# U's second half with every tile 512 columns wide: 16 narrow matmuls of each pair become 8 wide ones

## The chip, the core and the metric

The kernel runs on one core of one Trainium2 chip. The metric is device microseconds (us) of that core, lower is better. TensorE (PE) multiplies, its weight loads are listed apart as PEld; ScalarE (ACT), VectorE (DVE) and the DMA queue of SyncE (SP) stand beside it. Each engine executes its instructions in the order in which the built program lists them, and waits at an instruction until the semaphores that this instruction names have been raised.

## The reference, cut to what matters

A decoder layer with a mixer, and then a PEER layer over 16384 one-neuron experts, for 256 tokens. Only the last lines matter here:

```python
u = expert_u[eidx]
act = gelu(einsum('td,thkd->thk', xc, u))
out = einsum('thk,thkd->td', g * act, expert_v[eidx])
```

The kernel computes this densely: it multiplies x by every row of U, takes the GELU, multiplies by a gate that is zero for experts that a token has not chosen, and multiplies the result by V.

## The kernel before, in words

U is 16384 x 1024. It is read in 128 tiles of 128 experts by 1024 inputs, 512 KB each. A tile is computed as the sum of three products, because x and U are each split into a rounded high part and a low remainder: U_hi x_hi, U_hi x_lo and U_lo x_hi. The inputs go in eight chunks of 128, so one product is eight matmuls with 256 columns, one column for each token. The array `x2` holds the high and the low part of x side by side, 512 columns for each chunk.

There are two ways to do a tile.

- `dense` does 24 matmuls of 256 columns into one half of a PSUM bank: U_hi with x_hi, U_hi with x_lo, U_lo with x_hi.
- `u_wide` does U_hi with both halves of x at once: seven matmuls of 512 columns, then eight of 256 columns for U_lo with x_hi, then the eighth of 512 columns. The U_hi x_lo part then stands in the second half of the bank. ACT copies it to `ul` in SBUF, and DVE adds it to the first half.

The tiles of the first half (64, experts 0 to 63 of each group) all use `u_wide`. The second half is a loop of 32 pairs, n = 0 to 31. In a pair the even tile (r = 0) goes through `dense` straight into `pt[:, 0]`, and the odd tile (r = 1) through `u_wide` into a bank of its own, from which the add writes `pt[:, 1]`. Then ACT takes the GELU of `pt` in two pieces, and DVE multiplies one of them by the gates that are already in `act[1]`.

`gates(g, n)` makes the gates of eight tokens. DVE makes the one-hot rows `o1`, `eq` and `eq` times the gate weight; ACT makes eight scaled copies (line 1135), one for each token; PE multiplies 16 times (line 1141), two matmuls for each token, of which the second needs that token's scaled copy. DVE then multiplies the gates into `act[0]` and into the finished part of `act[1]` (line 1147), and ACT copies the rest (line 1149). There are 32 such groups. `spread` gives two to pair 0, two to pair 15, none to pairs 30 and 31, and one to each other pair. In the loop they are called in the middle of the even tile, between the U_hi and the U_lo matmuls.

All of this is written as a program without order across engines. A list scheduler of the framework places the instructions of each engine. PSUM has four banks for U tiles (`pbank`), and two for gates (`gbank`). `eq` has one buffer, `o1` and `o2` two, the split tiles `hi` and `lo` three, and `ul` one.

Of the kernel before, what the change touches and what calls it, by code (L numbers as in the profile page):

```python
# [20 lines left out]
T = 256  # L21
# [20 lines left out]
def f32(ap):  # L42
    return ap.bitcast(F32)
# [10 lines left out]
def layer(ctx, tc, I, out, tap=None, upto=None):  # L54
    nc = tc.nc
    V, S, P, PE = nc.vector, nc.scalar, nc.gpsimd, nc.tensor
# [5 lines left out]
    def load(src):  # L62
        raw = stream.tile([128, 1024], F32, tag="raw", bufs=RAWB, name="raw")
        nc.sync.dma_start(raw, src.rearrange("p a b -> p (a b)") if len(src.shape) == 3 else src)
        return raw

    def split(raw, eng=V, hi=None, lo=None):
        if hi is None:
            hi = stream.tile([128, 1024], F32R, tag="hi", bufs=HIB, name="hi")
            lo = stream.tile([128, 1024], F32R, tag="lo", bufs=LOB, name="lo")  # L70
        S.copy(hi, raw)  # L71
        eng.tensor_tensor(lo, raw, f32(hi), op=OP.subtract)  # L72
        return hi, lo

    def split3(raw):
        hi, lo = (stream.tile([128, 1024], F32R, tag=t, bufs=n, name=t)
                  for t, n in (("hi", HIB), ("lo", LOB)))
        S.copy(hi, raw)  # L78
        return hi, lo, V.tensor_tensor(lo, raw, f32(hi), op=OP.subtract)  # L79
# [22 lines left out]
    def pbank(shape):  # L102
        return ps.tile(shape, F32, tag="w", bufs=4, name="pw")
# [4 lines left out]
    def abank(shape):  # L108
        return ps0.tile(shape, F32, tag="a", bufs=2, name="pa")
# [3 lines left out]
    with ExitStack() as px:  # L113
# [6 lines left out]
        with ExitStack() as mx:  # L120
# [16 lines left out]
            pt = pbank([128, 512])  # L137
# [634 lines left out]
            for k in (4, 5, 6, 7):  # L772
                if k == 5:
                    r = sb.tile([128, 2, 1024], F32R, tag="qk", name="W5")
                    W[k] = split(load(I["w_out"][:, k, :]), V, r[:, 0], r[:, 1])
                elif k in LATE:
                    r = W3[:, 2 * (k - 6):2 * (k - 6) + 2]
# [7 lines left out]
            for k in range(2):  # L785
                r = sb.tile([128, 2, 1024], F32R, tag="Kin", name="W1") if k else W3[:, 0:2]
# [13 lines left out]
            xh, xl = x2[:, :, 0], x2[:, :, 1]  # L800
# [42 lines left out]
            for q in range(4):  # L843
# [6 lines left out]
                if q < 2:  # L850
                    r = late.tile([128, 2, 1024], F32R, tag="W4", bufs=2, name="W4")
                    hi, lo = r[:, 0], r[:, 1]
                else:
                    hi, lo = (stream.tile([128, 1024], F32R, tag=t, bufs=n, name=t)
                              for t, n in (("hi", HIB), ("lo", LOB)))
# [47 lines left out]
    HALF = NK // 2  # L903
# [4 lines left out]
    def of_tile(half, i):  # L908
        return act[half][:, i // 2, :, i % 2]

    def u_wide(i, dst, pt, pool, bufs):


        hi, lo, low = split3(load(I["u"][i]))
        for d in range(ND - 1):
            PE.matmul(pt, hi[:, 128 * d:128 * d + 128], x2[:, d], start=d == 0, stop=False)  # L916
        for d in range(ND):
            PE.matmul(pt[:, 0], lo[:, 128 * d:128 * d + 128], xh[:, d], start=False, stop=False)  # L918
        PE.matmul(pt, hi[:, D - 128:], x2[:, ND - 1], start=False, stop=True)  # L919
        ul = pool.tile([128, T], F32, tag="ul", bufs=bufs, name="ul")  # L920
        S.copy(ul, pt[:, 1])  # L921
        V.tensor_tensor(dst, pt[:, 0], ul, op=OP.add)  # L922
        return low


    with ExitStack() as rx:
# [24 lines left out]
        for hc in range(4, 16):  # L951
            raw = load(I["w_q"][hc])
            if hc == 4:
                with tc.issue_after(w4dma.ins):
                    nc.sync.dma_start(keys, I["keys"])
            hi, lo = (stream.tile([128, 1024], F32R, tag=t, bufs=n, name=t)
                      for t, n in (("hi", HIB), ("lo", LOB)))
# [4 lines left out]
            pt = abank([128, 2, T])[:, 0]  # L962
# [14 lines left out]
        def gbank(shape):  # L977
            return ps2.tile(shape, F32, tag="g", bufs=2, name="pg")
# [70 lines left out]
        def weigh():  # L1049

            S.activation(df, df, AF.Exp)
            for _ in range(2):
                yield
            sm = sb.tile([128, 2, 8], F32, name="sm")
            V.tensor_reduce(sm, df, axis=AX.X, op=OP.add)
            V.reciprocal(sm, sm)
            V.tensor_tensor(gn.rearrange("p b (h k) -> p b h k", k=16), df,
                            sm[:, :, :, None].to_broadcast([128, 2, 8, 16]), op=OP.mult)
            yield
            for b in range(2):  # L1060
                pt = gbank([128, 3, 128])
                for i, s in enumerate((i1n, i2n, gn)):
                    PE.transpose(pt[:, i], s[:, b], ident)
                sl = slice(128 * b, 128 * b + 128)
                V.tensor_copy(i1T[:, sl], pt[:, 0])
                V.tensor_copy(i2T[:, sl], pt[:, 1])

                gr = sb.tile([128, 128], F32, tag="gr", bufs=1, name="gr")
                V.tensor_scalar(gr, pt[:, 2], GSC, None, op0=OP.mult)
                V.tensor_copy(gT[:, sl], gr)  # L1070
                V.tensor_sub(gL[:, sl], gr, gT[:, sl])
                if tap:
                    tap(f"i1n{b}", i1n[:, b]); tap(f"gn{b}", gn[:, b])
                yield
# [3 lines left out]
        steps, last = chain(route(0), route(1)), weigh()  # L1078
# [18 lines left out]
    gk = ctx.enter_context(tc.tile_pool(name="gk", bufs=1))  # L1097
# [19 lines left out]
    def gates(g, done):  # L1117
        t0 = GT * g
        t = slice(t0, t0 + GT)

        sh = [128, GT // 2, 128, 2]
        o1 = gk.tile(sh, F16, tag="o1", bufs=2, name="o1")
        eq = gk.tile(sh, F16, tag="eq", bufs=1, name="eq")
        o2 = gk.tile([128, 2] + sh[1:], F16, tag="o2", bufs=2, name="o2")
        io = iotaq[:, None].to_broadcast(sh)

        def over(x):
            return x.rearrange("p (a b) -> p a b", b=2)[:, :, None, :].to_broadcast(sh)

        V.tensor_tensor(o1, io, over(i1T[:, t]), op=OP.is_equal)  # L1130
        V.tensor_tensor(eq, io, over(i2T[:, t]), op=OP.is_equal)  # L1131
        V.tensor_tensor(o2[:, 0], eq, over(gT[:, t]), op=OP.mult)

        for i in range(GT):
            S.activation(o2[:, 1, i // 2, :, i % 2], eq[:, i // 2, :, i % 2], AF.Copy,  # L1135
                         scale=gL[:, t0 + i:t0 + i + 1])

        pt = gbank([128, GT, 128])
        for i in range(GT):
            for k in range(2):  # L1140
                PE.matmul(pt[:, i], o1[:, i // 2, :, i % 2], o2[:, k, i // 2, :, i % 2],  # L1141
                          start=k == 0, stop=k == 1)
        gp = pt.rearrange("p t (i r) -> p t i r", r=2)
        for h, n in ((0, HALF // 2), (1, done)):
            if n:
                a = act[h][:, 0:n, t].rearrange("p i t r -> p t i r")
                V.tensor_tensor(a, gp[:, :, HALF // 2 * h:HALF // 2 * h + n], a, op=OP.mult)  # L1147
        if done < HALF // 2:
            S.copy(act[1][:, done:, t].rearrange("p i t r -> p t i r"), gp[:, :, HALF // 2 + done:])

    def spread(n, total, done):

        return min(total, -(-total * (n + 1) // done))

    made = 0
    for n in range(HALF // 2):

        due = spread(n, T // GT, HALF // 2 - 2)

        pt = pbank([128, 2, T])  # L1160
        hi, lo = split(load(I["u"][HALF + 2 * n]))
        dense(PE, pt[:, 0], hi, lo, xh, xl, beside=lambda: [gates(g, n) for g in range(made, due)])
        made = due
        u_wide(HALF + 2 * n + 1, pt[:, 1], pbank([128, 2, T]), gk, 1)
        a = act[1][:, n].rearrange("p t r -> p r t")
        m1 = GT * made
        if m1 < T:
            S.activation(a[:, :, m1:], pt[:, :, m1:], AF.Gelu_apprx_tanh)
        raw = gk.tile([128, T, 2], F32, tag="ga", bufs=2, name="ga").rearrange("p t r -> p r t")
        S.activation(raw[:, :, :m1], pt[:, :, :m1], AF.Gelu_apprx_tanh)  # L1170
        V.tensor_tensor(*(x[:, :, :m1].rearrange("p r t -> p t r") for x in (a, a, raw)), op=OP.mult)
# [39 lines left out]
    last, st = [], {}  # L1211
# [34 lines left out]
    for n, (c0, c1) in enumerate(PIECES):  # L1246
        p = pbank([128, 256]) if n else acc[1][:, 0]
        for i in range(LAST):
            hi, lo, wh, wl = last[i]
# [4 lines left out]
    ln_apply(1, 256, PIECES)  # L1254


def dense(PE, pt, hi, lo, xh, xl, last=None, beside=None):

    order = [(hi, xh), (hi, xl), (lo, xh)]
    if last is xl:  # L1260
        order = [(hi, xh), (lo, xh), (hi, xl)]
    for n, (w, x) in enumerate(order):
        for d in range(ND):
            PE.matmul(pt, w[:, 128 * d:128 * d + 128], x[:, d], start=n == 0 and d == 0,  # L1264
                      stop=n == 2 and d == ND - 1)
        if beside is not None and n == 1:
            beside()


def stats(nc, pool, st, b, z, n=512):  # L1270
# [90 lines left out]
```

## Time and profile before

| what | us |
|---|---|
| median of three runs | 951.42 (950.58 to 951.55) |
| profiled execution, its own time | 949.16 |
| span of that execution in the trace | 947.4 |
| PE busy, share of the span | 934.4, 99% |
| second half of U, from 375.70 to 589.40 | 213.70 |

The trace begins with the mixer. The first half of U ends at 375.70, the second half at 589.40, and V follows. The rows below are from the chain of waits, from the timeline and from groups of instructions; a number such as 1.61 stands for microseconds, where a row names ns it says so.

### The profile page before, as it was taken

The numbers are of one execution on the slowest core, as the hardware profiler recorded it, in microseconds if no ns is written. First come the engines' busy times: TensorE is split into PE (matmuls) and PEld (weight loads), VectorE is DVE, ScalarE is ACT, GpSimd is POOL, SyncE is SP. The second block draws the span as 40 slices with busy tenths as digits, with TensorE's granted clock in tenths as the row PEclk, the third lists the DMA queues.
The fourth block names the chain that finished last, engine by engine and source line by source line (L and its number), as shares of the span: only waits on it lengthen the run. The fifth ranks groups of instructions, "written<-read, shape, count | busy, mean of one in ns | idle before, by whom it ended". The sixth has DMA issues, their size and how long they took to land.

```text
span 947.4 us, 15305 instructions
## 1 busy us (share of the span) xinstructions
PE 934.4 (99%) x5588; PEld 810.0 (86%) x5588; DVE 721.7 (76%) x1495; ACT 562.8 (59%) x1067; POOL 11.2 (1%) x19
## 2 busy tenths in 40 slices
PE   9999999999999999999999999999999999999996
PEld 4887889998888888999999999888888888888885
DVE  9998687998988967888898996655555555555566
ACT  4526644566575667998888776554455465445550
POOL 3000010000000000000000000000000000000000
PEclk9999999999999999999999999999999999999998
DMA  7331573356555555354444445655555585555551
GB/s 290 111 113 58 173 237 112 135 179 202 195 180 198 182 195 178 134 182 156 156 157 156 157 157 178 198 189 192 198 192 190 196 285 188 193 200 189 191 198 45
DMA packets 50075, 166.18 MB, mean 175 GB/s; under 512 B 5328, under 2 KB 9936, under 8 KB 49872
## 3 DMA queue, kind: packets, MB, share of 16 engines
q1 hardware_dynamic: 50000, 165.20, 51.3%
q8 instruction: 44, 0.72, 0.3%
q14 instruction: 31, 0.25, 0.1%
HBM read 163.09 MB, written 2.10 MB: 174 GB/s over the span
## 4 chain that ended last, share of the span: by engine, by line
PE 91%; DVE 8%; issue 1%; ACT 0%; DVEq 0%; ACTq 0%
PE pg L1180 36%; PE pw L916 16%; PE pw L1264 10%; PE pw L918 10%; PE pg L1141 3%; PE pa L1264 3%; PE pw L919 2%; PE pw L768 2%; PE psb L217 1%; PE pa L871 1%; PE pw L623 1%; PE pw L498 1%; PE psb L552 1%; PE pw L648 1%; PE pw L945 0%
## 5 line engine op out<-in xcount | busy, mean ns | idle before, releaser
L72 DVE TENSOR_TENSOR lo<-raw,hi 128x1024 fp32r<-128x1024 f32 x168 | 205.6, 1224 | 151.8 <-ACT hi L71 151.6
L71 ACT CAST hi<-raw 128x1024 fp32r<-128x1024 f32 x168 | 176.9, 1054 | 171.8 <-PE pg L1180 156.5
L1180 PE MATMUL pg<-hi,wv 128*128 128x512 f32 x988 | 264.5, 389 | 0.0
L1180 PEld LDWEIGHTS pg<-hi,wv 128*128 128x128 f32 x988 | 185.4, 188 | 38.7 <-DVE wv L1111 0.2
L916 PE MATMUL pw<-x,hi 128*128 128x512 f32 x672 | 171.2, 393 | 0.0
L1180 PE MATMUL pg<-lo,wv 128*128 128x512 f32 x494 | 152.3, 389 | 0.0
L916 PEld LDWEIGHTS pw<-x,hi 128*128 128x128 f32 x672 | 124.3, 189 | 23.2
L79 DVE TENSOR_TENSOR lo<-raw,hi 128x1024 fp32r<-128x1024 f32 x96 | 117.1, 1219 | 16.8 <-ACT hi L78 15.8
L918 PEld LDWEIGHTS pw<-x,lo 128*128 128x128 f32 x768 | 104.8, 190 | 7.4
L1180 PEld LDWEIGHTS pg<-lo,wv 128*128 128x128 f32 x494 | 92.7, 188 | 19.2
L918 PE MATMUL pw<-x,lo 128*128 128x256 f32 x768 | 107.3, 282 | 0.0
L78 ACT CAST hi<-raw 128x1024 fp32r<-128x1024 f32 x96 | 101.2, 1054 | 4.2 <-PE pa L1264 2.7
L921 ACT COPY ul<-pw 128x256 f32<-128x256 f32 x96 | 35.6, 371 | 90.1 <-PE pw L919 90.1
L1135 ACT ACTIVATE o<-eq,gL 128x128 f16<-128x128 f16 x256 | 84.3, 439 | 6.0 <-DVE eq L1131 5.4
L1264 PEld LDWEIGHTS pw<-x,hi 128*128 128x128 f32 x512 | 65.9, 189 | 1.3
L1264 PE MATMUL pw<-x,hi 128*128 128x256 f32 x512 | 66.6, 283 | 0.0
L1110 ACT CAST wv<-act 128x256 fp32r<-128x256 f32 x125 | 52.3, 419 | 0.8 <-DVE act L1147 0.8
L1111 DVE TENSOR_TENSOR wv<-act,wv 128x256 fp32r<-128x256 f32 x125 | 52.0, 417 | 0.0
L1264 PE MATMUL pw<-x,lo 128*128 128x256 f32 x256 | 38.8, 292 | 0.0
L919 PE MATMUL pw<-x,hi 128*128 128x512 f32 x96 | 38.0, 396 | 0.0
L1141 PE MATMUL pg<-o,o 128*128 128x128 f16 x512 | 36.5, 219 | 0.0
L922 DVE TENSOR_TENSOR us<-pw,ul 128x256 f32<-128x256 f32 x64 | 26.8, 418 | 11.7 <-ACT ul L921 10.9
(341 smaller groups left out, 1121.0 us busy)
## 6 DMA issues: line engine op xcount, KB each, us to landing
raw<-in_u SPq DMA_DIRECT2D x128, 512.0 KB, 3.5
raw<-in_v SPq DMA_DIRECT2D x128, 512.0 KB, 3.4
raw<-in_w_q SPq DMA_DIRECT2D x12, 512.0 KB, 4.1
raw<-in_w_in SPq DMA_DIRECT2D x8, 512.0 KB, 6.2
raw<-in_w_out SPq DMA_DIRECT2D x8, 512.0 KB, 4.1
w<-in_w_in SPq DMA_DIRECT2D x7, 512.0 KB, 8.5
raw<-in_w_q SPq DMA_DIRECT2D x8, 256.0 KB, 4.9
raw<-in_w_glu SPq DMA_DIRECT2D x2, 512.0 KB, 3.4
```

Of the source, the lines that this page charges most:

```text
L71: S.copy(hi, raw)
L72: eng.tensor_tensor(lo, raw, f32(hi), op=OP.subtract)
L78: S.copy(hi, raw)
L79: return hi, lo, V.tensor_tensor(lo, raw, f32(hi), op=OP.subtract)
L916: PE.matmul(pt, hi[:, 128 * d:128 * d + 128], x2[:, d], start=d == 0, stop=False)
L918: PE.matmul(pt[:, 0], lo[:, 128 * d:128 * d + 128], xh[:, d], start=False, stop=False)
L919: PE.matmul(pt, hi[:, D - 128:], x2[:, ND - 1], start=False, stop=True)
L1110: S.copy(wh, of_tile(half, i))
L1135: S.activation(o2[:, 1, i // 2, :, i % 2], eq[:, i // 2, :, i % 2], AF.Copy, scale=gL[:, t0 + i:t0 + i + 1])
L1141: PE.matmul(pt[:, i], o1[:, i // 2, :, i % 2], o2[:, k, i // 2, :, i % 2], start=k == 0, stop=k == 1)
L1180: PE.matmul(acc[b][:, c], x[:, tk], w[:, 512 * c:512 * c + 512], start=first and j == 0, stop=last and j == 2)
L1264: PE.matmul(pt, w[:, 128 * d:128 * d + 128], x[:, d], start=n == 0 and d == 0, stop=n == 2 and d == ND - 1)
```

## The change

The even tile goes through `u_wide` as well. `u_wide` gets an argument `beside`, which is called behind its seven wide matmuls, and the gates of the pair are made there. Each pair now takes three PSUM banks for tiles (`pt` and one for each tile), where it took two. `dense` loses its argument `beside`.

```diff
-    def u_wide(i, dst, pt, pool, bufs):
+    def u_wide(i, dst, pt, pool, bufs, beside=None):
         hi, lo, low = split3(load(I["u"][i]))
         for d in range(ND - 1):
             PE.matmul(pt, hi[:, 128 * d:128 * d + 128], x2[:, d], start=d == 0, stop=False)
+        if beside:
+            beside()
         for d in range(ND):
             PE.matmul(pt[:, 0], lo[:, 128 * d:128 * d + 128], xh[:, d], start=False, stop=False)
         PE.matmul(pt, hi[:, D - 128:], x2[:, ND - 1], start=False, stop=True)
...
         pt = pbank([128, 2, T])
-        hi, lo = split(load(I["u"][HALF + 2 * n]))
-        dense(PE, pt[:, 0], hi, lo, xh, xl, beside=lambda: [gates(g, n) for g in range(made, due)])
+        for r in range(2):
+            u_wide(HALF + 2 * n + r, pt[:, r], pbank([128, 2, T]), gk, 1,
+                   (lambda: [gates(g, n) for g in range(made, due)]) if r == 0 else None)
         made = due
-        u_wide(HALF + 2 * n + 1, pt[:, 1], pbank([128, 2, T]), gk, 1)
...
-        if beside is not None and n == 1:
-            beside()
```

The lines of the changed kernel stand two further on: 918 becomes 920, 921 becomes 923, 1135 becomes 1137, 1141 becomes 1143, 1149 becomes 1151.

First place: PE at the start of the second half. Line 1264 before, and 916 to 921 after, are tile matmuls; `o_4124` and `o_4157` are the one-hot rows of the first and the second group before, `o_4116` and `o_4149` those after. Rows of the same group that only repeat are left out at "...". Before:

```order
L1264 MATMUL pw<-x_1230,hi 128x256 x16
L1141 MATMUL pg<-o_4126,o_4124 128x128
...
L1264 MATMUL pw<-x_1230,lo 128x256 x4
L1141 MATMUL pg<-o_4159,o_4157 128x128
L1264 MATMUL pw<-x_1230,lo 128x256 x4
L1141 MATMUL pg<-o_4159,o_4157 128x128
...
L916 MATMUL pw<-x_1230,hi 128x512
L1141 MATMUL pg<-o_4159,o_4157 128x128
...
L916 MATMUL pw<-x_1230,hi 128x512 x3
```

After:

```order
L916 MATMUL pw<-x_1230,hi 128x512 x7
L1143 MATMUL pg<-o_4118,o_4116 128x128
...
L920 MATMUL pw<-x_1230,lo 128x256 x7
L1143 MATMUL pg<-o_4151,o_4149 128x128
...
L920 MATMUL pw<-x_1230,lo 128x256
L921 MATMUL pw<-x_1230,hi 128x512
L1143 MATMUL pg<-o_4151,o_4149 128x128
...
L916 MATMUL pw<-x_1230,hi 128x512 x7
```

Before, the second group's matmuls were mixed with those of the odd tile; now nine of them stand in the even tile, and the other seven between the even tile and the odd one, all ahead of the odd tile's first matmul.

Second place: ACT in the same stretch, in the changed kernel, from the GELU of the first half's last pair (line 989) to the third and fourth group (`o2_4241`, `o2_4332`). `ul_4191` and `ul_4282` are the copies of the even tiles of pairs 0 and 1, `ul_4217` that of pair 0's odd tile.

```order
L989 ACTIVATE act0_1460<-us_4029 128x2x256
L1137 ACTIVATE o2_4151<-eq_4150,gL_66 128x128 x6
L1151 COPY act1_4097<-pg_4130 128x8x32x2
L1137 ACTIVATE o2_4151<-eq_4150,gL_66 128x128 x2
L923 COPY ul_4191<-pw_4102 128x256
...
L1137 ACTIVATE o2_4241<-eq_4240,gL_66 128x128 x7
L923 COPY ul_4217<-pw_4194 128x256
L1137 ACTIVATE o2_4241<-eq_4240,gL_66 128x128
L78 CAST hi_4319<-raw_4317 128x1024
L1169 ACTIVATE act1_4097<-pw_4101 128x2x240
L1171 ACTIVATE ga_4221<-pw_4101 128x2x16
L1137 ACTIVATE o2_4332<-eq_4331,gL_66 128x128 x6
L923 COPY ul_4282<-pw_4225 128x256
```

In the kernel before, a cast (`L78 CAST hi_4296`) stood between the GELU and the second group's copies; the copies of the even tiles, `ul_4191` and `ul_4282`, are new, and on PE 15 matmuls of the fourth group have moved ahead of pair 1's odd tile.

Third place: ACT in pair 26, late in the loop, in the changed kernel. `ul_6526` is the copy of the tile before, `ul_6591` the new copy of this pair's even tile, `o2_6641` a group of gates of which PE takes the first ten matmuls between this pair's even and odd tile.

```order
L923 COPY ul_6526<-pw_6503 128x256
L78 CAST hi_6628<-raw_6626 128x1024
L1169 ACTIVATE act1_4097<-pw_6442 128x2x32
L1171 ACTIVATE ga_6530<-pw_6442 128x2x224
L1137 ACTIVATE o2_6641<-eq_6640,gL_66 128x128 x2
L1151 COPY act1_4097<-pg_6562 128x8x6x2
L1137 ACTIVATE o2_6641<-eq_6640,gL_66 128x128 x2
L923 COPY ul_6591<-pw_6534 128x256
L1137 ACTIVATE o2_6641<-eq_6640,gL_66 128x128 x4
```

The fifth scaled copy of the group has moved behind the even tile's copy; before, a group's matmuls stood in the middle of the even tile of its own pair, behind eight finished scaled copies.

## Rows read from the trace of the kernel before

**Rows 1.** The page: span, and busy time of each engine.

```profile
span 947.4 us, 15305 instructions
PE 934.4 (99%) x5588; PEld 810.0 (86%) x5588; DVE 721.7 (76%) x1495; ACT 562.8 (59%) x1067; POOL 11.2 (1%) x19
```

**Rows 2.** The page: the chain that ended last, by engine.

```profile
PE 91%; DVE 8%; issue 1%; ACT 0%; DVEq 0%; ACTq 0%
```

**Rows 3.** Windows of eight pairs: stretch, length, busy of PE, PEld, DVE, ACT, POOL, clock, DMA.

```profile
394.70:447.93 53.23, 53.23 (x450) 50.17 (x449) 47.59 (x77) 48.90 (x124) 0.00 (x0) 1.00 0.50 170
501.07:554.29 53.22, 53.22 (x449) 50.16 (x449) 48.71 (x73) 43.07 (x113) 0.00 (x0) 1.00 0.46 159
```

**Rows 4.** Chain of waits in order of time: start, us, what; one pair, and the end.

```profile
390.85 1.92 PE pw L1264 x16
392.77 0.94 PE pg L1141 x16
393.70 1.00 PE pw L1264 x8
394.70 1.61 PE pw L916 x7
396.32 0.95 PE pw L918 x8
397.27 0.23 PE pw L919
...
578.06 2.88 PE pw L1264 x24
...
589.40 50.79 PE pg L1180 x224
```

**Rows 5.** The same chain, the first two pairs of the second half.

```profile
375.70 1.91 PE pw L1264 x16
...
381.78 0.29 PE pw L916
...
383.98 2.28 PE pw L1264 x19
```

**Rows 6.** Timeline of ACT and DVE at the start: start, us, engine, line.

```profile
377.28 0.68 DVE L1131 TENSOR_TENSOR eq<-iotaq,i2T 128x1024 f16<-128x1024 f16 x1
377.69 0.68 ACT L987 ACTIVATE act<-us 128x512 f32<-128x512 f32 x1
378.26 1.03 ACT L78 CAST hi<-raw 128x1024 fp32r<-128x1024 f32 x1
378.82 0.68 DVE L1147 TENSOR_TENSOR act<-pg,act 128x512 f32<-128x512 f32 x1
385.30 0.60 ACT L1168 ACTIVATE act<-pw 128x480 f32<-128x480 f32 x1
```

**Rows 7.** Timeline of ACT and DVE in later pairs.

```profile
390.94 0.37 ACT L921 COPY ul<-pw 128x256 f32<-128x256 f32 x1 [0.26 <-PE pw L919]
391.35 0.43 DVE L922 TENSOR_TENSOR pw<-pw,ul 128x256 f32<-128x256 f32 x1
416.19 1.91 ACT L1135 ACTIVATE o<-eq,gL 128x128 f16<-128x128 f16 x6
418.20 1.06 ACT L71 CAST hi<-raw 128x1024 fp32r<-128x1024 f32 x1
419.15 0.54 ACT L1168 ACTIVATE act<-pw 128x400 f32<-128x400 f32 x1
```

**Rows 8.** The page: the scaled copies, busy us, mean ns of one, idle before.

```profile
L1135 ACT ACTIVATE o<-eq,gL 128x128 f16<-128x128 f16 x256 | 84.3, 439 | 6.0 <-DVE eq L1131 5.4
```

**Rows 9.** Groups by form on ACT, late pairs: shape, count, busy us, mean ns.

```profile
L1170 ACT ACTIVATE ga<-pw 128x448 f32<-128x448 f32 x1 | 0.6, 589 | 0.0
L1168 ACT ACTIVATE act<-pw 128x80 f32<-128x80 f32 x1 | 0.2, 240 | 0.0
L1149 ACT COPY act<-pg 128x96 f32<-128x96 f32 x1 | 0.2, 245 | 0.0
```

More of the change, by code (lines that the diff above doesn't have):

```diff
@@ L1254, in layer, with dense @@
     ln_apply(1, 256, PIECES)
-def dense(PE, pt, hi, lo, xh, xl, last=None, beside=None):
+def dense(PE, pt, hi, lo, xh, xl, last=None):
     order = [(hi, xh), (hi, xl), (lo, xh)]
```

## The prediction, made before the changed kernel ran

> **What bounds the kernel now.** I read the page first: PE is busy for 934.4 of 947.4 us [rows 1], and the chain that ended last is 91% PE [rows 2]. So PE's time is the kernel's time, and the question is how PE's chain in the second half of U gets shorter or breaks. The chain in order of time shows a pair there as six unbroken pieces [rows 4]: 16 narrow matmuls 1.92, 16 gate matmuls 0.94, eight narrow 1.00, seven wide 1.61, eight narrow 0.95, one wide 0.23, together 6.65. The reader should see that no piece waits. The windows show why this is fragile: in eight pairs (53.23 us) DVE is busy for 47.59 to 48.71 and ACT for 48.90 early and 43.07 late [rows 3], so both stand at 81 to 92%, and both execute in order.
>
> **What the change saves on PE.** A narrow matmul costs 1.92 / 16 = 0.120, a wide one 1.61 / 7 = 0.230 [rows 4]. A wide one does the columns of two narrow ones for 0.01 less. By pair: the odd tile takes 1.61 + 0.95 + 0.23 = 2.79, and an even tile without gates takes 2.88 [rows 4]; both now take 2.79.
> Not all of it stays. Where a wide matmul follows gate matmuls it takes 0.29 in place of 0.23 [rows 5], and the eight narrow ones behind gates take 1.00 in place of 0.95. In the new order a group is often cut into two blocks, one in the even tile and one ahead of the odd one; I count 48 blocks. Sum for the stage without any wait: 64 tiles x 2.79 = 178.6, 32 groups x 0.94 = 30.1, 48 x 0.06 = 2.9, together 211.5. Now it is 589.40 - 375.70 = 213.70 [rows 4, 5]. The saving is **2.2 us**.
> Here the Trainium skill can be weighed. The page "TensorE: Matmul & The Clock Gate", section "Back-to-back issue gap", gives a gap of N / 2.4 + 2.5 ns for a matmul of N columns, 109 ns for 256 and 216 ns for 512. An estimate by that page would be 16 x 109 - 8 x 216 = 16 ns for a pair, 0.5 us in all, in place of 2.2. The rows give 0.120 and 0.230, so the trace stands above both figures, and I keep the rows.
>
> **What it adds beside PE.** Each even tile gets a copy `ul` on ACT (0.37) and an add on DVE (0.43) [rows 7], 32 of each. By engine time there is still room: ACT 48.90 / 8 + 0.37 = 6.48 early, DVE 48.71 / 8 + 0.43 = 6.52 late, against 211.5 / 32 = 6.61 for PE. So on average they stay hidden, with almost nothing to spare. The third PSUM bank costs nothing by itself: the odd tile's bank was last freed by an add of the pair before, the even one's by the GELU of the pair before, which ends some 2 us behind the pair, and PE can take only the older one of these a whole tile later.
>
> **What moves.** The order shows the real cost. Gates of the next pair now stand on PE between the even tile and the odd one. A gate matmul that waits for its scaled copy holds back the whole odd tile, where before the eight scaled copies were finished long ahead. What is late next is ACT's queue: casts, GELUs and the new copy stand ahead of the scaled copies. ACT's own pace: an instruction starts 0.11 before the end of the one ahead (the cast at 418.20 lasts 1.06, the next starts at 419.15) [rows 7], and scaled copies follow each other every (1.91 - 0.44) / 5 = 0.294 [rows 7, 8]. A result reaches PE some 0.05 after its end, which I take from the add that starts 0.04 after the copy [rows 7].
>
> *Start, pair 0.* ACT is free for the second group at 378.26 (the cast that started there has moved [rows 6]). Six scaled copies take it to 380.02; the copy of line 1151, 512 columns, which I take as the GELU of 512 columns, 0.68 less 0.11 [rows 6], to 380.6; the eighth scaled copy starts at 380.9 and ends at 381.3. PE without a wait would be through even tile and both groups at 375.70 + 2.79 + 1.87 + 0.1 = 380.46. It waits **0.9**, and pair 0 ends near 384.25.
> *Start, pair 1.* The third group's `eq` waits on DVE behind the multiply of the second group, which follows PE's last gate at 381.4: 0.2 until it starts, 0.60, an add 0.35, `eq` 0.68 [rows 6, 7], so 383.25. Seven scaled copies 2.06, the copy 0.26, one more 0.29, the cast 0.95, the GELU in two pieces 0.65 (480 columns take 0.60 [rows 6]), six of the fourth group 1.76, the copy of the even tile 0.26, and the seventh ends 0.44 later, at 389.9. PE is there at 384.25 + 2.79 + 0.94 + 0.06 + 15 x 0.058 = 388.9. It waits **1.1**.
> *Late, pair 26.* Count from the end of the tile before. The copy starts at 0.09 [rows 4, 7] and frees ACT at 0.35, the cast at 1.30; the add is done at 0.93, before that. The GELU pieces, 64 and 448 columns, take 0.14 and 0.48 (0.240 and 0.589 less 0.11 [rows 9]): 1.92. Two scaled copies 2.51, the copy of 96 columns 0.14 [rows 9]: 2.65, two more 3.24, the even tile's copy 3.50, and the fifth scaled copy ends at 3.94. PE's tenth gate matmul could start at 2.79 + 9 x 0.058 = 3.32 and starts at 3.99: it waits **0.65**.
> I went through the order of the other pairs in the same way. In pairs 16, 20, 22, 24 and 28 the last scaled copy that PE needs ahead of the odd tile also stands behind the even tile's copy on ACT, for 0.5 to 0.8 each; in the rest it stands ahead of that copy and PE finds it done. Together with pair 26 the late waits are **3.7**.
>
> **Sum.** -2.2 + 0.9 + 1.1 + 3.7 = +3.5 us. The profiled execution has a span of 947.4 and a time of 949.16; by the sum it becomes 950.9 and 952.7. The median of the runs is 951.42, 2.26 above that execution, so the median becomes **954.9**. Bounds of what is unknown: the late waits are nothing, if ACT reaches the copies 0.65 earlier than I count, and twice 3.7, if DVE, which has 0.1 to spare in a pair, delays the add by as much again; the waits at the start lie between 0 and 4. That gives -2.2 to +9.2, or 949.2 to 960.6.
>
> **The rivals.**
> *The saving only.* ACT runs ahead of PE by a whole group, as it does before in the late pairs, where it is idle for 10 of 53 us [rows 3], so that no gate matmul waits. Against it speak the in-order chains above: the GELU cannot start before the add, and the scaled copies stand behind the GELU. It decides if PE finds the fifth copy of pair 26 by 3.32. Time 951.42 - 2.2 = 949.2, faster.
> *The start waits and the late pairs don't*: -2.2 + 2.0 = -0.2, 951.2, no change. For it: a late error of only 0.65 in my count for six pairs. This is the same mechanism at half the price.
> *ACT and DVE become the bound throughout.* If their gaps of now (DVE 53.22 - 48.71 = 4.5 in eight pairs [rows 3]) stay and the add comes on top, a pair takes 6.65 + 0.43 - some 0.1, for 30 pairs +10 us: 961. Against it: a queue that is late loses its gaps first.
> *Fewer weight loads.* A pair has 32 tile loads in place of 40. If loads were the bound, as PEld's 50.17 of 53.23 [rows 3] may suggest, eight matmuls of 0.120 would vanish from each pair: 31 us, 920. Against it: a wide matmul takes 0.230 with one load [rows 4]. The page "Trainium Kernel Development and Optimization" of the Trainium skill, section "Best Practices", wants the distance to the roofline judged by the weight loads' busy share; by that rule this rival would hold, and the wide row contradicts it here.
>
> **Chances and range.** Waits at the start and late, 0.56; start only, 0.21; saving only, 0.12; ACT and DVE throughout, 0.09; weight loads, 0.02. A measurement tells about 0.2% (1.9 us) from no change. The likeliest case gives 952.5 to 958, of which the lowest part is no change. Slower 0.61, same 0.25, faster 0.14. The range takes the start-only case and most of the wider bounds: 950.3 to 959.6.
>
> **What would show each step right or wrong.** In the profile after: wide matmuls at 0.230 and a tile at 2.79 in the chain; the saving is wrong if that differs. PE should show idle time ahead of gate matmuls (line 1143), released by ACT's scaled copies (line 1137): about 1 us in each of pairs 0 and 1, and 0.5 to 0.8 in pairs 16, 20, 22, 24, 26 and 28; other pairs should take 6.5 to 6.6. If PE waits at a tile's first matmul instead, it is PSUM or the casts, and my reading of the banks is wrong. If there are no waits and the stage takes 211.5, the first rival holds. What would make the prediction wrong most easily is ACT's lead at the start of a pair, which I took as free at the end of PE's tile.

## The result, and the profile after

The changed kernel takes 956.9 us (median of four runs, 956.19 to 957.92) against 951.0 us (four runs of the kernel before beside it, 950.18 to 951.55): a ratio of 1.0067, 95% interval 1.0055 to 1.0080. It is slower by 5.9 us; predicted were 954.9 (950.3 to 959.6), which is 3.5 us slower than before. The page of the profiled execution, its own time 957.92 (a row of part 5 names line, engine, operation and tiles, then busy us, mean ns, and the idle time before with its releaser):

```profile
span 955.8 us, 14805 instructions
...
PE 938.7 (98%) x5332; PEld 794.1 (83%) x5332; DVE 732.5 (77%) x1527; ACT 571.2 (60%) x1099; POOL 11.2 (1%) x19
...
PE 80%; DVE 11%; ACT 8%; issue 1%; DMA 0%; DVEq 0%; ACTq 0%
...
L916 PE MATMUL pw<-x,hi 128*128 128x512 f32 x896 | 229.3, 395 | 0.0
...
L1143 PE MATMUL pg<-o,o 128*128 128x128 f16 x512 | 43.0, 220 | 3.2 <-ACT o L1137 2.7
```

PE has 256 matmuls and as many weight loads less than in [rows 1], and the kernel is slower all the same. The line with the shares says where: the chain that ended last was 91% PE, 8% DVE and 0% ACT [rows 2], and is now 80%, 11% and 8%. PE's recorded idle time stands ahead of the gate matmuls (line 1143), and mostly the scaled copies (line 1137) end it; ahead of the wide matmuls (line 916) there is none. The chain in order of time shows a pair without a wait (from 430.59) and the end of a wait in pair 1 (columns as in [rows 4]):

```profile
390.63 0.22 ACT ul L923
390.84 0.35 ACT o L1137
391.19 0.04 issue
391.23 0.28 PE pg L1143 x2
391.51 1.67 PE pw L916 x7
...
430.59 0.93 PE pg L1143 x16
431.52 1.67 PE pw L916 x7
433.19 0.94 PE pw L920 x8
434.13 0.23 PE pw L921
434.36 1.61 PE pw L916 x7
435.97 0.95 PE pw L920 x8
436.92 0.23 PE pw L921
```

A tile costs 1.61 + 0.95 + 0.23 = 2.79, and 1.67 in place of 1.61 behind gate matmuls, as I had taken it from [rows 4, 5]. In pair 1 the chain comes from ACT's copy of the even tile (line 923) and the scaled copy behind it (line 1137) to PE's last two gate matmuls (line 1143), and only then does the odd tile begin.

**How the waits are measured.** The profile models the ends of matmuls, so the idle time in a row is too small: 3.2 for line 1143 above, where the starts give 8.3. I take the starts: matmuls that follow each other start 0.230 (512 columns), 0.120 (256) or 0.058 (128) apart, and where a distance exceeds that by more than 0.1, the excess is counted as a wait. PE's and ACT's timeline of the changed kernel, in pair 0, pair 16 and pair 26:

```profile
381.54 0.40 PE L1143 MATMUL pg<-o,o 128*128 128x128 f16 x4
382.40 0.51 PE L1143 MATMUL pg<-o,o 128*128 128x128 f16 x3 [0.46 <-ACT o L1137]
...
491.65 1.48 PE L1143 MATMUL pg<-o,o 128*128 128x128 f16 x9
493.69 0.51 PE L1143 MATMUL pg<-o,o 128*128 128x128 f16 x3 [0.56 <-ACT o L1137]
...
561.52 0.75 ACT L1137 ACTIVATE o<-eq,gL 128x128 f16<-128x128 f16 x2
561.63 0.97 PE L1143 MATMUL pg<-o,o 128*128 128x128 f16 x9
562.12 0.38 ACT L923 COPY ul<-pw 128x256 f32<-128x256 f32 x1
562.37 1.33 ACT L1137 ACTIVATE o<-eq,gL 128x128 f16<-128x128 f16 x4
562.89 0.22 PE L1143 MATMUL pg<-o,o 128*128 128x128 f16 x1 [0.29 <-ACT o L1137]
```

In pair 0 four matmuls start from 381.54 on, so the next could start at 381.77; it starts at 382.40. In pair 26 the tenth gate matmul (562.89) needs the fifth scaled copy, the first of the four at 562.37, which stand behind the even tile's copy (562.12). The whole stage, by pair (us):

```
where (pair)         predicted   measured in the trace
0                    0.9         0.97
1                    1.1         1.10
16                   0.5-0.8     2.25
20, 22, 24, 26, 28   0.5-0.8     0.80, 0.60, 0.60, 0.72, 0.62
6, 14, 15, 18        none        0.25, 0.13, 0.15, 0.14
all waits            5.7         8.3
stage, start of the first tile to the start of V
  before             213.8       (375.45 to 589.24)
  after              220.0       (376.86 to 597.56, less 0.7 for three V matmuls that lie inside)
```

The stage is 6.2 longer, about what the medians differ by. The two spans differ by 8.4; the rest is not of the change: 1.4 arises in the mixer (last section), and 0.8 in V, where the traces of e1, e4 and e9 below are longer than this one of before by as much, too.

### The profile page after: what moved, and what is told of

It reads as the page before. It is cut to its first block, busy times and chain, and to the rows that moved or that the text cites. A ratio compares the mean times of both kernels' runs of the same rounds, so it can differ in the third digit from the quotient of the medians.

```text
span 955.8 us, 14805 instructions
## 1 busy us (share of the span) xinstructions
PE 938.7 (98%) x5332; PEld 794.1 (83%) x5332; DVE 732.5 (77%) x1527; ACT 571.2 (60%) x1099; POOL 11.2 (1%) x19
## 4 chain that ended last, share of the span: by engine, by line
PE 80%; DVE 11%; ACT 8%; issue 1%; DMA 0%; DVEq 0%; ACTq 0%
PE pg L1181 35%; PE pw L916 17%; PE pw L920 10%; ACT o L1137 3%; PE pa L1265 2%; PE pw L921 2%; ACT hi L78 2%; PE pw L768 2%; PE pg L1143 2%; PE psb L217 1%; PE pa L871 1%; DVE lo L79 1%; ACT ul L923 1%; PE pw L623 1%; PE pw L498 1%
## 5 line engine op out<-in xcount | busy, mean ns | idle before, releaser
L916 PE MATMUL pw<-x,hi 128*128 128x512 f32 x896 | 229.3, 395 | 0.0
L916 PEld LDWEIGHTS pw<-x,hi 128*128 128x128 f32 x896 | 166.3, 188 | 32.5 <-issue 0.6
L920 PEld LDWEIGHTS pw<-x,lo 128*128 128x128 f32 x1024 | 138.1, 190 | 8.9
L78 ACT CAST hi<-raw 128x1024 fp32r<-128x1024 f32 x128 | 135.0, 1055 | 2.8 <-PE pa L1265 2.7
L923 ACT COPY ul<-pw 128x256 f32<-128x256 f32 x128 | 47.4, 370 | 90.5 <-PE pw L921 87.8
L1137 ACT ACTIVATE o<-eq,gL 128x128 f16<-128x128 f16 x256 | 87.1, 441 | 8.6 <-DVE eq L1133 8.5
L921 PE MATMUL pw<-x,hi 128*128 128x512 f32 x128 | 50.6, 395 | 0.0
L1143 PE MATMUL pg<-o,o 128*128 128x128 f16 x512 | 43.0, 220 | 3.2 <-ACT o L1137 2.7
L1143 PEld LDWEIGHTS <-o 128*128 128x128 f16 x512 | 30.7, 97 | 15.7 <-issue 11.2
L1149 DVE TENSOR_TENSOR act<-pg,act 128x512 f32<-128x512 f32 (+29 forms) x62 | 32.4, 548 | 1.0 <-PE pg L1143 0.9
L924 DVE TENSOR_TENSOR pw<-pw,ul 128x256 f32<-128x256 f32 x64 | 27.5, 429 | 5.5 <-ACT ul L923 4.6
```

## The experiments

Ten kernels ran, each timed in five rounds beside the kernel before on the same chip. "Ratio to before" is against those runs. The waits and the stage are read from each trace as above. The expectations put the changed kernel at 956.6 or 956.7; its median is 956.9.

```
run                             median us   ratio to before, 95%      stage    waits
e1 two banks                    949.50      0.9983 [0.9974, 0.9992]   211.6     0.4
e2 three banks, order on PE     956.61      1.0063 [1.0049, 1.0076]   220.1     9.3
e3 narrow, three banks          965.22      1.0155 [1.0141, 1.0169]   228.3    14.4
e4 narrow, two banks            950.96      1.0004 [0.9995, 1.0013]   214.0     0.2
e5 one bank held                949.27      0.9981 [0.9971, 0.9991]   211.5     0.4
e6 gates ahead, two banks       954.77      1.0043 [1.0028, 1.0058]   217.8     6.8
e7 double load                  952.01      1.0009 [0.9999, 1.0019]   214.7     1.0
e8 two banks in pairs 0 and 1   957.18      1.0061 [1.0046, 1.0076]   219.4     7.4
e9 three banks, adds last       947.80      0.9968 [0.9957, 0.9979]   211.6     0.5
e10 one group a pair            954.32      1.0031 [1.0019, 1.0043]   217.8     5.9
```

(Where V matmuls lie inside the stage, three in e2, e8 and e10 and seven in e3, 0.23 for each is taken off. Of e6's 6.8, 0.9 is no wait but four matmuls at a lower clock, as the last section shows.)

**e1: the even tile's add writes its own bank.**

```diff
-            u_wide(HALF + 2 * n + r, pt[:, r], pbank([128, 2, T]), gk, 1,
+            u_wide(HALF + 2 * n + r, pt[:, r], pt if r == 0 else pbank([128, 2, T]), gk, 1,
```

> The changed kernel with one edit: the even tile's add writes back into the even tile's own PSUM bank, so a pair takes two banks in place of three. Every engine executes the same instructions of the same sizes; only their order changes: from pair 2 on the gate matmuls stand in the even tile of their own pair again, as before the change. Theory (the place of the gate matmuls makes PE wait): the waits ahead of gate matmuls go, 8.3 us of the changed kernel's stage, and the saving of 2.2 us stays; 951.0 - 2.2 = 948.8, within 948 to 950. Rival (the 32 copies and 32 adds make ACT and DVE the bound, wherever the gates stand): the pairs stay near (597.56 - 376.86) / 32 = 6.9 us and the time stays at 955 to 958.

949.50: the waits are gone and the saving is there (stage 211.6 against 213.8, 2.2 us; the medians differ by 1.0). The load of ACT and DVE as the bound is refuted, since the load is the same.

**e2: the place of the gates on PE alone.** Three banks stay; the gate matmuls are queued behind the even tile's wide ones.

```diff
-            PE.matmul(pt, hi[:, 128 * d:128 * d + 128], x2[:, d], start=d == 0, stop=False)
+            mm = PE.matmul(pt, hi[:, 128 * d:128 * d + 128], x2[:, d], start=d == 0, stop=False)
         if beside:
-            beside()
+            with tc.issue_after(mm.ins):
+                beside()
```

> The changed kernel with three banks for a pair, but with the gate matmuls held back in PE's order until the even tile's wide matmuls of their own pair; only pair 0 keeps seven gate matmuls ahead of its odd tile. Theory (the place of the gate matmuls): pair 0 still waits about 1.0 us, all other pairs do not; 951.0 - 2.2 + 1.0 = 949.8, within 949 to 951. Rival A (the third PSUM bank itself costs time): 954 or more, with idle time ahead of a tile's first matmul. Rival B (load of ACT and DVE): 955 to 958.

956.61. Pair 0 waits 0.97 as foreseen, but the theory fell: with the gates in place the time is lost elsewhere. The timeline of ACT, DVE and PE in a late pair:

```profile
520.65 2.20 ACT L1138 ACTIVATE o<-eq,gL 128x128 f16<-128x128 f16 x7 [0.21 <-DVE eq L1134]
...
522.72 0.35 ACT L924 COPY ul<-pw 128x256 f32<-128x256 f32 x1
...
523.09 0.43 DVE L925 TENSOR_TENSOR pw<-pw,ul 128x256 f32<-128x256 f32 x1 [0.75 <-ACT ul L924]
523.58 0.73 PE L916 MATMUL pw<-x,hi 128*128 128x512 f32 x2 [0.77 <-DVE pw L925]
```

The copy of the odd tile before stands on ACT behind seven scaled copies, DVE's add waits for it, and PE's next odd tile waits for the add, which reads the bank that it needs. Ten such waits, in pairs 19 to 28, make up most of the 9.3 us; at each of them PE starts within 0.1 of the end of that add. That looked like rival A, the third bank, and e5 and e9 were made to test it.

**e3 and e4: the added copy and add without wide matmuls.** The even tile stays narrow. In e3 it has a bank of its own, in e4 all is done in the pair's bank:

```diff
-        dense(PE, pt[:, 0], hi, lo, xh, xl, beside=lambda: [gates(g, n) for g in range(made, due)])
+        pe = pbank([128, 2, T])
+        dense(PE, pe[:, 0], hi, lo, xh, xl, beside=lambda: [gates(g, n) for g in range(made, due)])
+        ul = gk.tile([128, T], F32, tag="ul", bufs=1, name="ul")
+        S.activation(ul, pe[:, 0], AF.Copy, scale=0.0)
+        V.tensor_tensor(pt[:, 0], pe[:, 0], ul, op=OP.add)
```

(e4: `pt` in place of `pe` throughout.)

> The kernel before, even tile still in 24 narrow matmuls, but into a bank of its own, with a copy on ACT (scaled by zero, 256 columns) and an add on DVE that writes the pair's bank, as the wide even tile has them; the result is the same. The gate matmuls then stand between the even and the odd tile again, up to 21 at once. Theory (the place of the gate matmuls): no wide matmul is needed for the loss; PE's own time for a pair stays 6.65, and it waits for scaled copies as in the changed kernel, 8.3 us less what 0.13 us more of PE's time in a pair gives ACT; 951.0 + 4 to 8.5 = 955 to 959.5. Rival (the loss belongs to the wide matmuls): 951, no change.

> The kernel before with the same extra copy on ACT (0.37 us) and add on DVE (0.43 us) in each pair, but in the pair's bank itself; the gate matmuls stay in the even tile as before. Theory (order, not load): ACT has 48.90 / 8 + 0.37 = 6.48 and DVE 48.71 / 8 + 0.43 = 6.52 of PE's 6.65 in a pair, so both stay hidden; 951.0, within 950 to 952.5. Rival (load of ACT and DVE alone makes PE wait): as in the changed kernel some 8 us of waits, 955 or more; half of it if 0.13 us more of PE's time helps, 953 to 955.

e4 shows no change: the load alone costs nothing. e3 loses 14.7 us, more than I expected, without one more wide matmul. The list of PE's waits in e3 (recorded idle time, so again less than the starts give; us in total, times, longest):

```profile
PE pg L1141 <- ACT act L1149: 5.1, 9, 0.8
PE pg L1141 <- ACT o L1135: 2.5, 8, 0.5
```

Besides the scaled copies (line 1135) PE waits nine times for ACT's copy of the gates out of PSUM (line 1149): up to 21 gate matmuls stand ahead of the odd tile there, and the next group's begin before its PSUM tile is free.

**e5: one bank for all odd tiles.** Beside e1's edit:

```diff
+    held = pbank([128, 2, T])
+    V.tensor_copy(held[:, 0, 0:8], gL[:, 0:8])
     made = 0
...
+    keep = gk.tile([128, 8], F32, tag="keep", bufs=1, name="keep")
+    V.tensor_tensor(keep, held[:, 0, 0:8], act[1][:, HALF // 2 - 1, 0:8, 0], op=OP.add)
     acc = [gbank([128, 2, 512]) for _ in range(2)]
```

> The kernel of e1 (two banks for a pair, gate matmuls in the even tile of their own pair), but one of the four PSUM banks is held from the start of the loop to its end by eight columns that are written before it and read behind it; the result is the same. Every odd tile then goes into one and the same bank, as in e2, and may start only when the add of the pair before has read it. In e1 that add ended 4.9 to 10.3 us behind its tile and nobody waited; with one bank for the odd tiles only the even tile and a group of gates lie between, 2.79 + 0.94 = 3.7 us. Theory (the third bank takes away the distance by which ACT and DVE may lag behind PE): waits at the odd tile's first matmul, released by the add, as in e2 with its 9.3 us; 955 to 959. Rival (the loss of the changed kernel comes from the place of the gate matmuls, and e2's from something in its own order): 949 to 950.5, as e1.

949.27, as e1: the bank theory fell as well. A figure in this expectation and in e8's was misread: I had paired adds with the wrong tiles. Read again, with a tile's end at 0.23 behind the start of its last matmul, e1's adds end 1.0 to 2.6 us behind their tiles, and e5's odd ones 1.0 to 1.9; in e2 the odd ones end up to 4.8 behind. A single bank for the odd tiles allows 3.7, so it costs nothing as long as ACT and DVE come to the add in time, and in e2 they don't.

**e6: gates ahead of the odd tile, in every pair, with two banks.** The core of the edit (`ahead` is called ahead of the odd tile's first matmul, which is queued behind the last gate matmul):

```diff
+        nxt = spread(n + 1, T // GT, HALF // 2 - 2)
...
+        u_wide(HALF + 2 * n, pt[:, 0], pt, gk, 1, (lambda: [gates(g, n) for g in range(made, due)]) if n == 0 else None)
+        u_wide(HALF + 2 * n + 1, pt[:, 1], pbank([128, 2, T]), gk, 1, None, early)
+        made = nxt
```

> The kernel of e1 with two banks for a pair, but each group's 16 gate matmuls stand ahead of the odd tile of the pair before, in one block, as the changed kernel has many of them; pair 0 gets its third group there, too. The GELU's two pieces are cut eight tokens later, nothing else changes. Theory (banks, not the gates' place): a wait of about 3.5 us in pair 0, where the third group is not ready (its one-hot rows start near 383.2 and eight scaled copies at 0.294 follow, 386.3, while PE is there near 382.6), none in the steady pairs; 949.5 + 3.5 = 953, within 951.5 to 954.5. Rival (a gate matmul ahead of the odd tile waits for its scaled copy in many pairs, with two banks too): 0.5 to 0.8 in six or more pairs on top of the start, 956 to 959.

954.77, a little above the range of the theory. The third group's wait in pair 0 is 3.61, as worked out (the 0.97 of the changed kernel's pair 0 stands ahead of it), and the steady pairs have none: from pair 2 to pair 13 no distance exceeds its usual value. So the place ahead of the odd tile is harmless where ACT's order fits it. Two things came on top: 1.3 us of waits in pairs 14 and 15, at the double group, and PE's clock after its long wait (last section).

**e7: the added load twice.** Beside e1's edit, behind both tiles:

```diff
+        ul = gk.tile([128, T], F32, tag="ul", bufs=1, name="ul")
+        S.activation(ul, pt[:, 0], AF.Copy, scale=0.0)
+        V.tensor_tensor(pt[:, 0], pt[:, 0], ul, op=OP.add)
```

> The kernel of e1 with the added load doubled: a second copy on ACT (0.37 us) and a second add on DVE (0.43 us) in each pair, the copy scaled by zero, so that the result is the same. ACT then has 48.90 / 8 + 2 x 0.37 = 6.85 and DVE 48.71 / 8 + 2 x 0.43 = 6.95 of PE's 6.61 in a pair. If room on the engines is what counts beyond 6.61 (theory: the change itself is just below this point), the pairs stretch towards 6.95: up to 30 x 0.34 = 10 us, less what the lag that two banks allow takes up at first; 954 to 960. If ACT and DVE still have room that the busy times don't show: 949 to 951.

952.01, between the two: the load costs something when it is doubled, but a quarter of what I had worked out. From pair 2 to pair 19 the pairs take 6.58 as in e1 (pair 15, with two groups, 7.49); pairs 20 to 28 take 6.6 to 7.8. What is left is hardly a wait (1.0 us in all). PE's timeline in pair 26:

```profile
556.16 0.47 PE L1143 MATMUL pg<-o,o 128*128 128x128 f16 x5
556.44 0.48 PE L916 MATMUL pw<-x,hi 128*128 128x512 f32 x1
556.76 0.29 PE L1143 MATMUL pg<-o,o 128*128 128x128 f16 x2
```

The scheduler has cut this pair's gates into blocks of one to five, and a wide matmul between two blocks takes 556.76 - 556.44 = 0.32 to the next start in place of 0.23.

**e8: e1's edit in pairs 0 and 1 alone** (`pt if r == 0 and n < 2 else pbank(...)`).

> The changed kernel, with the even tile's add in its own bank in pairs 0 and 1 alone; from pair 2 on three banks. The waits of pairs 0 and 1 were 0.97 and 1.10 us in the changed kernel's trace. If they are a term by themselves (as in my sum): 956.6 - 2.1 = 954.5, within 953.5 to 955.2. If ACT and DVE only come later by as much (in e1 the adds of pairs 0 and 1 ended 8 to 10 us behind their tiles) and three banks don't allow that from pair 2 on, the time is waited there: 956 to 957.5.

957.18, no gain. The waits of pairs 0 and 1 are gone but for 0.17, but pair 2 now waits 1.37 and pair 17 1.60, pairs 9, 11 and 13, free in the changed kernel, wait 0.37 to 0.57, and the later waits sit in pairs 19, 21, 23, 25 and 27 in place of 18, 20, 22, 24, 26 and 28. The terms of my sum are not independent: an order that begins otherwise runs out of step elsewhere.

**e9: three banks, the copies and adds named behind both tiles.** `u_wide` hands back its last two instructions as `finish`:

```diff
-        pt = pbank([128, 2, T])
-        for r in range(2):
-            u_wide(HALF + 2 * n + r, pt[:, r], pbank([128, 2, T]), gk, 1,
-                   (lambda: [gates(g, n) for g in range(made, due)]) if r == 0 else None)
+        parts = [u_wide(HALF + 2 * n + r, None, pbank([128, 2, T]), gk, 1,
+                        (lambda: [gates(g, n) for g in range(made, due)]) if r == 0 else None, True)
+                 for r in range(2)]
+        pt = pbank([128, 2, T])
+        for r in range(2):
+            parts[r](pt[:, r])
```

> The changed kernel with three banks for a pair, but the program names the matmuls of both tiles first and then the two copies and adds, so that the pair's bank is taken behind the odd tile's. From pair 2 on PE's order is that of e1, with the gate matmuls in the even tile of their own pair. Theory (the order that the scheduler makes is the cause; three banks and the added copy and add are not): as e1, 949.5, within 948.5 to 950.5, with the adds 1 to 4 us behind their tiles. Rival (three banks for a pair cost time by themselves): 954 to 957.

947.80, 3.5 us under the kernel before beside it (951.31; 0.32% by the ratio, 0.21 to 0.43). The chain in order of time in a late pair of e9:

```profile
516.60 1.61 PE pw L916 x7
518.20 0.94 PE pg L1148 x16
519.14 1.01 PE pw L920 x8
520.15 0.23 PE pw L921
520.38 1.61 PE pw L916 x7
521.99 0.95 PE pw L920 x8
522.94 0.23 PE pw L921
```

6.58 and unbroken, with the gates in the middle of the even tile, where [rows 4] gives 6.65. The page of e9 counts the same instructions on every engine as that of the changed kernel (PE 5332, DVE 1527, ACT 1099); only their order differs, and it is worth 8.4 us of the stage (220.0 against 211.6); the medians differ by 9.1.

e9's order is no new one. Through the whole run PE, ACT and DVE execute the same sequence of instructions in e9 as in e1 (compared by operation and tile name, without buffer numbers), and PE's starts in the stage agree within 0.03 us. So e1 and e9 are one good order with two banks and with three. Both beat the kernel before; the distance between their medians is not of this change, nor is what e9's median gains beyond the 2.2 us of the stage.

**e10: no double group in pair 15** (`spread(n, T // GT, HALF // 2 - 1)`).

> The changed kernel with one number changed: the 32 groups of gates are spread over 31 pairs in place of 30, so that pair 15 gets one group like the others and pair 30 gets one, too; pair 0 keeps two. In the changed kernel's trace pair 16, behind the two groups of pair 15, waits 2.25 us, where I had counted 0.5 to 0.8. If the double group is what made my count of pair 16 too small, this wait goes and the others stay: 956.7 - 2.25 = 954.5, within 953.5 to 955.3. If pair 16 waits for the reason that the other late pairs have, one wait of about 0.6 stays there: 956.7 - 1.65 = 955.0 at least; if the backlog only moves to a later pair: 956 to 957.

954.32. Pair 16 waits 0.43 in place of 2.25. The other waits stay where they were, but pair 26 waits 0.27 in place of 0.72, with nine gate matmuls ahead of its odd tile in place of ten, and pair 15 none: 5.9 in all, 2.4 less. So the double group made pair 16 dear, and a wait of the common kind stays there.

## Why the prediction was right, and which terms were mis-sized

- *The saving of 2.2* is right: 213.8 - 211.6 in e1 and in e9, with 0.4 and 0.5 of waits in it. In the changed kernel the stage without its waits is 211.7, where I had 211.5.
- *The start, 0.9 and 1.1*: measured 0.97 and 1.10, at the instructions named.
- *The late waits, 3.7*: the six pairs are the right ones, and five of them (20 to 28) give 3.34, where I had counted some 3.1. **Pair 16 is the mis-sized term**: 2.25 in place of some 0.6, and it makes most of the 2.6 us by which all waits exceed the predicted 5.7. I had treated it as one of six alike. The chain goes through DVE and ACT there from 482.43 to 493.65 without returning to PE, and the two groups of pair 15 put four multiplications of line 1149 on DVE (to 484.68) ahead of the next one-hot rows, where e10 has two there and waits 1.8 less. Four pairs that I had called free add 0.67. So the sum gave +3.5 where the stage shows +6.2 and the medians +5.9: right in kind and place, too small by the late waits.
- *The third bank costs nothing by itself*: right. e9 runs e1's order with three banks in e1's time; e5, with one bank for all odd tiles, loses nothing either.
- *Hidden on average, with almost nothing to spare*: hidden is right (e1, e4), the margin was too narrow. I added whole durations, 0.37 and 0.43, but a copy takes 0.25 of ACT's queue (562.12 to 562.37 above), and by the two pages ACT's busy time grew by 8.4 us and DVE's by 10.8, 0.26 and 0.34 a pair. In e1 ACT is busy for 48.87 of 52.40 early and DVE for 51.20 of 53.00 late, or 6.14 and 6.36 of a pair of 6.58, where I had 6.48 and 6.52:

```profile
395.60:448.00 52.40, 52.40 (x384) 45.61 (x384) 48.45 (x82) 48.87 (x127) 0.00 (x0) 1.00 0.52 171
501.00:554.00 53.00, 53.00 (x389) 46.16 (x389) 51.20 (x82) 45.54 (x119) 0.00 (x0) 1.00 0.52 170
```

- *The cause*: "a gate matmul that waits for its scaled copy holds back the whole odd tile" is what the changed kernel's trace shows, but it is the face of the loss and not its root. e2 takes that face away and loses as much at another place, and e6 has the gates ahead of every odd tile without a wait in the steady pairs. The root is the order that the scheduler gave to all engines together: e9 has the instructions and the three banks of the changed kernel and only another order, and the loss is gone. In these kernels the order came out bad where the even tile has a bank of its own and the add that empties it stands ahead of the odd tile's matmuls in the program, and good where that add stays in the tile's own bank or is named behind both tiles. Why the scheduler plans this way I did not measure; that in its plan the odd tile waits until the pair's bank is taken is my reading of the order, not shown. Which part of the order costs e2 its time is argued, not isolated: PE's order there is e9's but for pairs 0, 1, 17 and 28 and the last, the odd tiles share a bank as e5's edit makes them do, and neither e9 nor e5 loses. What is left is mainly the order on ACT and DVE, which differs from e9's.
- *The rivals*: saving only is what e1, e5 and e9 are (949.2 predicted for it). Start only is refuted by the changed kernel's late pairs (5.6 us of waits in the six). ACT and DVE throughout is refuted by e1 and e4. Fewer weight loads are refuted by the changed kernel itself: PEld fell from 810.0 [rows 1] to 794.1, and a wide matmul still takes 0.230.

## What to carry to other kernels

When a list scheduler places the instructions, a change is three things: its arithmetic, its load on each engine, and the order that falls out; only the first two can be read from the diff. Here they gave -2.2 us, and the order gave +8.3 of waits, which e9 took back by naming the same instructions in another sequence. So compare the orders of all engines that wait for each other, not only of the busiest, before believing a saving; and where an order is bad, try that before adding edges that hold one engine (e2).

## What the runs showed of the hardware

**PE's clock after a long wait.** In e6 PE stood nearly idle from 381.5 to 385.03. The windows of e6 (columns as in [rows 3]) and PE's timeline behind the wait:

```profile
382.00:385.20 3.20, 0.17 (x2) 0.17 (x3) 3.20 (x6) 2.90 (x9) 0.00 (x0) 0.98 0.53 164
385.20:387.00 1.80, 1.80 (x17) 1.80 (x16) 1.55 (x3) 1.04 (x4) 0.00 (x0) 0.50 0.81 271
387.00:388.60 1.60, 1.60 (x5) 1.22 (x5) 1.41 (x3) 1.60 (x6) 0.00 (x0) 0.53 0.06 23
388.60:390.00 1.40, 1.40 (x11) 1.28 (x10) 0.47 (x1) 0.90 (x3) 0.00 (x0) 1.00 0.00 0
```

```profile
385.03 1.88 PE L1147 MATMUL pg<-o,o 128*128 128x128 f16 x16 [3.45 <-DVE o L1138]
386.67 2.69 PE L918 MATMUL pw<-x,hi 128*128 128x512 f32 x7
```

When PE came back the granted clock was 0.50, its level of 1.2 GHz, until about 388.6. The 16 gate matmuls took (386.67 - 385.03) / 16 = 0.10 each in place of 0.058, and the first four wide ones together 0.92 more than at 0.230: some 1.6 us that are no waits. By the starts the 0.92 looks like one and is counted in e6's 6.8; the granted clock tells the two apart. In the changed kernel, whose longest wait is 0.7, the granted clock is 1.00 in every window of the stage that I looked at. The page "TensorE: Matmul & The Clock Gate" of the Trainium skill, section "What's actually happening", knows only this level and 2.4 GHz and puts the lower one down to idling; the trace agrees, with 3.45 of idling ahead of it and a granted clock of 1.00 again from 388.6 on.

**A step of 1.4 us far from the change.** The row of ACT in the mixer where the spans part, first before, then the changed kernel:

```profile
65.61 1.05 ACT L71 CAST hi<-raw 128x1024 fp32r<-128x1024 f32 x1 [7.79 <-PE psb L217]
```

```profile
67.03 1.05 ACT L71 CAST hi<-raw 128x1024 fp32r<-128x1024 f32 x1 [9.21 <-PE psb L217]
```

The program is the same there, and in the twelve traces the second half of U begins either at 375.4 to 375.7 or at 376.8 to 377.1, with nothing between. What decides it is open; it is as large as a quarter of the effect, so the stages were compared and not the spans. How many of the timed runs had the longer mixer is not known, since only one execution of each kernel was traced.
